# Two weight sums made by an accumulating DMA, and seven products in ten of sixteen weight pairs

## The chip, the cores and the metric

The kernel runs on one core of a Trainium2 chip. The metric is the device time of one execution in microseconds (us). The core has five instruction queues that this text names as the profile does: PE (matmuls), DVE and ACT (element-wise work), POOL and SP (which here mostly start DMAs). Each queue runs its instructions in the order in which the program holds them; an instruction that has to wait holds up everything behind it on its queue.

## What is computed

One encoder layer on 256 frames of 4096 channels: a layer norm, one wide projection, a retention branch and a forgetting-attention branch, a gated merge, an output projection and a last layer norm. Cut to what costs time:

```
h = layer_norm(x, ln_in_g, ln_in_b)                       # 256 x 4096
proj = h @ w_in                                           # 4096 x 24592, most of the work
q_r, k_r, v_r, g_r, q_f, k_f, v_f, g_f, f, gates = split(proj)
y_r = group_norm(retention(rotary(q_r), rotary(k_r), v_r)) * silu(g_r)
y_f = forgetting_attention(q_f, k_f, v_f, f + b_forget) * silu(g_f)
merged = sigmoid(gates0) * (y_r @ w_branch_ret) + sigmoid(gates1) * (y_f @ w_branch_fox)
out = layer_norm(2**0.25 * h + merged @ w_out, ln_post_g, ln_post_b)
```

All is float32. The kernel splits each operand of a large product into a high and a low float32r part and adds three matmuls: high times high, high times low, low times high (`three`, L197 to L200).

## The kernel before

**The column pairs.** 20480 of the projection's columns are done as 20 column pairs of 1024 columns each (L885 to L888). For one column pair the 4096 channels are run through in 16 steps of 256. The code calls such a step a pair: two blocks of 128 channels by two blocks of 512 columns, so four weight blocks of 128 x 512, which the code calls b11, b12, b21 and b22; the other operand is two blocks of 128 channels by two of 128 frames.

**Eight or seven products.** A plain pair takes eight block products of three matmuls each, 24 matmuls. The pairs in `SEVEN` (8 to 15) use Winograd's form of Strassen's scheme: seven products, 21 matmuls, but with four sums of activation blocks, made once (`make_sops`, L361), and four sums of weight blocks, made anew for every pair and column pair by DVE: `ta` holds t1 and t3 (L184, one instruction of 1024 columns), `tb` holds t2 and t4 (L186 and L187, 512 columns each). Each sum is then split, the high part by an ACT cast and the low part by a DVE subtraction (`split_into`, L152), into the tile `tset`. Three more splits are needed for the raw blocks. The products add up in eight PSUM tiles over the 16 pairs; then ACT copies them out (`proj_evac`, L389) and DVE combines them (`combine`).

**Buffers.** Weights come as one DMA of 1 MB for each pair, issued by SP into one of three `wraw` buffers (`u_load`, L133). The split blocks lie in two sets of slots, used in turn, the sums' parts in two `tset` tiles, used in turn (yb0 and yb1). The activation sums of eight pairs fill yb2 and yb3.

**Order.** `PAIRS` takes a plain and a seven-product pair in turn: 0, 8, 1, 9 and so on. The code issues the splits of a pair as soon as the slots it needs are free in the code's own reckoning (`feed`, `slots_for`), and the next load after that (`load_more`). A list scheduler then sets each queue's final order, so matmuls of neighbouring pairs stand interleaved.

Of the kernel before, what the change touches and what calls it, by code (L numbers as in the profile page):

```python
# [8 lines left out]
F32 = mybir.dt.float32  # L9
# [4 lines left out]
P = 128  # L14
# [15 lines left out]
SEVEN = tuple(range(8, 16))  # L30
GATE0, GATE1 = 7, 15
PAIRS = tuple(p for i in range(8) for p in (i, 8 + i))
# [3 lines left out]
def hybrid_kernel(  # L36
# [29 lines left out]


    xt = []
    for t in range(T):
        xt.append(big.tile([P, D], F32, name=f"x{t}", tag=f"yb{t}"))  # L70
# [86 lines left out]
    def u_split(u):  # L157
# [15 lines left out]
        B = [raw[:, i * NC:(i + 1) * NC] for i in range(4)]  # L173
        st = [tuple(w_tile(s_, i) for i in range(2)) for s_ in u["slots"][:2]]
        if not u["seven"]:
            for i in range(2):
                split_into(st[i][0], st[i][1], raw[:, 2 * i * NC:2 * (i + 1) * NC])
            u["b"] = [(st[i // 2][0][:, i % 2 * NC:(i % 2 + 1) * NC], st[i // 2][1][:, i % 2 * NC:(i % 2 + 1) * NC])
                      for i in range(4)]
            return  # L180
        split_into(st[0][0], st[0][1], raw[:, NC:3 * NC])
        ta = work.tile([P, 2, NC], F32, name="ta", tag="w4a", bufs=1)
        tb = work.tile([P, 2, NC], F32, name="tb", tag="w4b", bufs=1)
        nc.vector.tensor_tensor(ta, B[0][:, None, :].to_broadcast([P, 2, NC]),  # L184
                                raw[:, NC:3 * NC].rearrange("p (a n) -> p a n", a=2), op=ALU.add)
        nc.vector.tensor_tensor(tb[:, 0, :], ta[:, 0, :], B[2], op=ALU.add)  # L186
        nc.vector.tensor_tensor(tb[:, 1, :], tb[:, 0, :], B[3], op=ALU.add)  # L187
        split_into(st[1][0][:, :NC], st[1][1][:, :NC], B[3])
        ts = big.tile([P, 2, 2, 2, NC], F32R, name="tset", tag="yb0" if u["slots"][2] == "t0" else "yb1")
        for i, t_ in enumerate((ta, tb)):  # L190
            split_into(ts[:, i, 0], ts[:, i, 1], t_)
        two = lambda x, i: (x[0][:, i * NC:(i + 1) * NC], x[1][:, i * NC:(i + 1) * NC])
# [24 lines left out]
    def pair_pe(u):  # L217
# [11 lines left out]
        if u["seven"]:  # L229
# [3 lines left out]
            work_ = [("1", blk(0, 0), f["b11"]), ("2", blk(0, 1), f["b21"]), ("6", so(2), f["t2"]),  # L233
                     ("5", so(1), f["t1"]), ("3", so(0), f["b22"]), ("7", so(3), f["t3"]), ("4", blk(1, 1), f["t4"])]
# [126 lines left out]
    def make_sops(hi, lo, pairs_, sops):  # L361
        sh = big.tile([P, len(pairs_), 4, P], F32R, name="soh", tag="yb2")
# [765 lines left out]
```

## Time and profile before

| | us |
|---|---|
| median of 3 runs | 2848.74 (2847.06 to 2856.11) |
| the profiled execution, its own time | 2845.76 |
| its span, from first to last instruction | 2844.0 |
| PE busy | 2793.1 (98%) |
| DVE busy | 2305.3 (81%) |
| ACT busy | 1565.1 (55%) |
| POOL busy | 169.8 (6%) |

The column pairs take the stretch from about 131 to 1749 us, 57% of the span. The granted TensorE clock is 1.00 there, the higher of its two levels. A matmul's own duration (0.39 us) is longer than the distance to the next one, since they overlap; what a matmul costs is read from how many start in a stretch.

### The profile page before, as it was taken

The numbers are of one execution on the slowest core, as the hardware profiler recorded it, in microseconds if no ns is written. First come the engines' busy times: TensorE is split into PE (matmuls) and PEld (weight loads), VectorE is DVE, ScalarE is ACT, GpSimd is POOL, SyncE is SP. The second block draws the span as 40 slices with busy tenths as digits, with TensorE's granted clock in tenths as the row PEclk, the third lists the DMA queues.
The fourth block names the chain that finished last, engine by engine and source line by source line (L and its number), as shares of the span: only waits on it lengthen the run. The fifth ranks groups of instructions, "written<-read, shape, count | busy, mean of one in ns | idle before, by whom it ended". The sixth has DMA issues, their size and how long they took to land. (4 is left out here: it accounts for less than half of the span.)

```text
span 2844.0 us, 34687 instructions
## 1 busy us (share of the span) xinstructions
PE 2793.1 (98%) x12666; PEld 2308.8 (81%) x12666; DVE 2305.3 (81%) x2988; ACT 1565.1 (55%) x2170; POOL 169.8 (6%) x302
## 2 busy tenths in 40 slices
PE   7999999999999999999999999999999999999998
PEld 5788888888887887888878888788898888888886
DVE  7899999998999988989889888877675656656666
ACT  5565666656555655555555565445664444444443
POOL 1000000000000000000000000212220000000000
PEclk9999999999999999999999999999999999999999
DMA  6556655665566655556656656866676566666564
GB/s 221 198 207 239 225 219 214 230 224 205 214 222 222 222 211 211 211 211 222 222 213 218 221 204 224 290 229 202 204 232 216 211 215 211 226 215 231 210 233 170
DMA packets 128156, 620.28 MB, mean 218 GB/s; under 512 B 15803, under 2 KB 16075, under 8 KB 87019
## 3 DMA queue, kind: packets, MB, share of 16 engines
q1 hardware_dynamic: 105552, 543.47, 52.8%
q0 software_dynamic: 21856, 72.49, 8.2%
q8 instruction: 99, 1.62, 0.2%
q10 hardware_dynamic: 576, 2.10, 0.2%
q14 instruction: 73, 0.60, 0.1%
HBM read 588.54 MB, written 29.46 MB: 217 GB/s over the span
## 5 line engine op out<-in xcount | busy, mean ns | idle before, releaser
L153 ACT CAST whi<-wraw 128x1024 fp32r<-128x1024 f32 (+1 forms) x640 | 586.3, 945 | 373.7 <-PE ps L200 262.1
L154 DVE TENSOR_TENSOR wpart<-wraw,wpart 128x512 fp32r<-128x512 f32 (+2 forms) x790 | 520.4, 667 | 314.0 <-ACT wpart L153 311.9
L153 ACT CAST wpart<-wraw 128x512 fp32r<-128x512 f32 (+2 forms) x790 | 475.3, 606 | 525.5 <-DVE wpart L154 314.4
L154 DVE TENSOR_TENSOR wlo<-wraw,whi 128x1024 fp32r<-128x1024 f32 (+1 forms) x640 | 680.8, 1084 | 8.7 <-ACT whi L153 7.2
L199 PE MATMUL ps<-wlo,hTh 128*128 128x512 f32 x960 | 373.7, 389 | 0.0
L200 PE MATMUL ps<-whi,hTl 128*128 128x512 f32 x960 | 373.4, 389 | 0.0
L198 PE MATMUL ps<-whi,hTh 128*128 128x512 f32 x960 | 340.2, 390 | 5.8 <-ACT ev L397 5.6
L184 DVE TENSOR_TENSOR ta<-wraw 128x1024 f32<-128x1024 f32 x160 | 195.6, 1222 | 137.6 <-DMA wraw<-in_w_in 136.5
L153 ACT CAST tset<-tb 128x1024 fp32r<-128x1024 f32 x160 | 169.3, 1058 | 183.8 <-DVE tb L187 183.6
L199 PE MATMUL acc<-wlo,hTh 128*128 128x512 f32 x640 | 249.1, 391 | 3.4 <-DVE wlo L154 3.4
L200 PE MATMUL acc<-whi,hTl 128*128 128x512 f32 x640 | 247.8, 389 | 0.0
L198 PE MATMUL acc<-whi,hTh 128*128 128x512 f32 x640 | 242.2, 389 | 0.4 <-ACT whi L153 0.4
L153 ACT CAST tset<-ta 128x1024 fp32r<-128x1024 f32 x160 | 167.6, 1048 | 120.1 <-DVE ta L184 119.8
L198 PEld LDWEIGHTS ps<-whi,hTh 128*128 128x128 f32 x960 | 180.2, 188 | 46.4 <-ACT ev L397 9.1
L199 PE MATMUL acc<-wpart,hTh 128*128 128x512 f32 (+2 forms) x568 | 212.2, 377 | 4.2 <-DVE wpart L154 4.1
L200 PEld LDWEIGHTS ps<-whi,hTl 128*128 128x128 f32 x960 | 180.2, 188 | 37.6
L199 PEld LDWEIGHTS ps<-wlo,hTh 128*128 128x128 f32 x960 | 180.2, 188 | 37.3
L200 PE MATMUL acc<-wpart,hTl 128*128 128x512 f32 (+2 forms) x568 | 208.2, 370 | 0.6 <-DVE rstd L96 0.6
L154 DVE TENSOR_TENSOR tset<-tb,tset 128x1024 fp32r<-128x1024 f32 x160 | 195.0, 1219 | 4.7 <-ACT tset L153 4.7
L154 DVE TENSOR_TENSOR tset<-ta,tset 128x1024 fp32r<-128x1024 f32 x160 | 194.8, 1217 | 0.4
L199 PE MATMUL acc<-wpart,mTh 128*128 128x512 f32 x500 | 194.6, 389 | 0.0
L200 PE MATMUL acc<-wpart,mTl 128*128 128x512 f32 x500 | 194.5, 389 | 0.0
(257 smaller groups left out, 4853.3 us busy)
## 6 DMA issues: line engine op xcount, KB each, us to landing
wraw<-in_w_in SPq DMA_DIRECT2D x320, 1024.0 KB, 4.9
wraw<-in_w_out SPq DMA_DIRECT2D x128, 512.0 KB, 4.1
wraw<-in_w_in SPq DMA_DIRECT2D x112, 512.0 KB, 4.8
wraw<-in_w_branch_ret SPq DMA_DIRECT2D x64, 512.0 KB, 4.2
wraw<-in_w_branch_fox SPq DMA_DIRECT2D x64, 512.0 KB, 4.2
proj_d<-ev POOLq DMA_DIRECT2D x64, 256.0 KB, 3.5
g<-gates_d POOLq DMA_DIRECT2D x16, 512.0 KB, 5.7
wraw<-in_w_in SPq DMA_DIRECT2D x16, 272.0 KB, 4.5
```

Source lines behind the costliest of these rows:

```text
L153: c = nc.scalar.copy(hi, src)
L154: nc.vector.tensor_tensor(lo, src, hi.bitcast(F32), op=ALU.subtract)
L184: nc.vector.tensor_tensor(ta, B[0][:, None, :].to_broadcast([P, 2, NC]), raw[:, NC:3 * NC].rearrange("p (a n) -> p a n", a=2), op=ALU.add)
L198: nc.tensor.matmul(o, lhsT=a[0], rhs=w[0], start=first, stop=False)
L199: nc.tensor.matmul(o, lhsT=a[0], rhs=w[1], start=False, stop=False)
L200: return nc.tensor.matmul(o, lhsT=a[1], rhs=w[0], start=False, stop=last)
```

## The change

Four things change together.

- Ten of the sixteen pairs (6 to 15) go by seven products, and `PAIRS` becomes 0, 6, 7, 1, 8, 9, 2, 10, 11, 3, 12, 13, 4, 14, 5, 15, so that seven-product pairs often follow each other.
- The sum `ta` is no longer made by DVE. The four weight blocks of such a pair are stored in another order. SP loads three of them (768 KB) into `wraw`; a second DMA on SP writes the fourth twice, side by side, into one half of a new tile `mix`; and an accumulating DMA on POOL adds two of the blocks, fetched again from memory, to it there.
- There is one `tset` instead of two, and its tile stays the same all along, so its quarters are released one by one. The seven products now start with those that use the sums (5, 7, 6, 4) and end with 1, 3, 2.
- The buffer that this frees, yb1, is cut in two: one half holds the activation sums of the two added pairs, the other holds `mix`, which is two `ta` buffers used in turn. `tb` gets two buffers too.

```diff
-SEVEN = tuple(range(8, 16))
+SEVEN = tuple(range(6, 16))
-PAIRS = tuple(p for i in range(8) for p in (i, 8 + i))
+PAIRS = (0, 6, 7, 1, 8, 9, 2, 10, 11, 3, 12, 13, 4, 14, 5, 15)
...
     def u_load(ld):
         raw = wp.tile([P, 4 * NC], F32, name="wraw", tag="wraw", bufs=RAW)
         w = ld["srcs"][0].shape[0] // P
+        if ld.get("seven"):
+
+            src = ld["srcs"][0].rearrange("(p f) -> p f", p=P)
+            nc.sync.dma_start(raw[:, :3 * NC], src[:, :3 * NC])
+            ta = scr["ta"][scr["n"] % 2]
+            scr["n"] += 1
+            nc.sync.dma_start(ta, src[:, None, 3 * NC:].to_broadcast([P, 2, NC]))
+            nc.gpsimd.dma_start(ta, src[:, :2 * NC].rearrange("p (a n) -> p a n", a=2), accum_op=ALU.add)
+            ld["raw"], ld["ta"] = raw, ta
+            return
...
-        split_into(st[0][0], st[0][1], raw[:, NC:3 * NC])
-        ta = work.tile([P, 2, NC], F32, name="ta", tag="w4a", bufs=1)
-        tb = work.tile([P, 2, NC], F32, name="tb", tag="w4b", bufs=1)
-        nc.vector.tensor_tensor(ta, B[0][:, None, :].to_broadcast([P, 2, NC]),
-                                raw[:, NC:3 * NC].rearrange("p (a n) -> p a n", a=2), op=ALU.add)
-        nc.vector.tensor_tensor(tb[:, 0, :], ta[:, 0, :], B[2], op=ALU.add)
-        nc.vector.tensor_tensor(tb[:, 1, :], tb[:, 0, :], B[3], op=ALU.add)
-        split_into(st[1][0][:, :NC], st[1][1][:, :NC], B[3])
-        ts = big.tile([P, 2, 2, 2, NC], F32R, name="tset", tag="yb0" if u["slots"][2] == "t0" else "yb1")
+        ta, ts = u["ld"]["ta"], scr["t"]
+        tb = work.tile([P, 2, NC], F32, name="tb", tag="w4b" if scr["s"] % 2 else "w4a", bufs=1)
+        scr["s"] += 1
+        nc.vector.tensor_tensor(tb[:, 0, :], ta[:, 0, :], raw[:, NC:2 * NC], op=ALU.add)
+        nc.vector.tensor_tensor(tb[:, 1, :], tb[:, 0, :], raw[:, 2 * NC:3 * NC], op=ALU.add)
         for i, t_ in enumerate((ta, tb)):
             split_into(ts[:, i, 0], ts[:, i, 1], t_)
+        split_into(st[0][0], st[0][1], raw[:, :2 * NC])
+        split_into(st[1][0][:, :NC], st[1][1][:, :NC], raw[:, 2 * NC:3 * NC])
...
-            work_ = [("1", blk(0, 0), f["b11"]), ("2", blk(0, 1), f["b21"]), ("6", so(2), f["t2"]),
-                     ("5", so(1), f["t1"]), ("3", so(0), f["b22"]), ("7", so(3), f["t3"]), ("4", blk(1, 1), f["t4"])]
+            work_ = [("5", so(1), f["t1"]), ("7", so(3), f["t3"]), ("6", so(2), f["t2"]), ("4", blk(1, 1), f["t4"]),
+                     ("1", blk(0, 0), f["b11"]), ("3", so(0), f["b22"]), ("2", blk(0, 1), f["b21"])]
...
-        sh = big.tile([P, len(pairs_), 4, P], F32R, name="soh", tag="yb2")
-        sl = big.tile([P, len(pairs_), 4, P], F32R, name="sol", tag="yb3")
+        so = [big.tile([P, 4, 2, 4, P], F32R, name="sop", tag=f"yb{2 + i}") for i in range(2)]
+        so.append(big.tile([P, 2, 2, 4, P], F32R, name="sop2", tag="yb1a"))
+        mix = big.tile([P, 4, NC], F32, name="mix", tag="yb1b")
+        scr["ta"] = mix[:, 0:2], mix[:, 2:4]
+        scr["t"] = big.tile([P, 2, 2, 2, NC], F32R, name="tset", tag="yb0")
...
         while state["loaded"] < min(len(loads), state["done"] + RAW):
+            if loads[state["loaded"]].get("seven") and "ta" not in scr:
+                break
             u_load(loads[state["loaded"]])
...
-            cands = [("r0", "r1") if (i - first_pair) % 2 else ("a0", "a1")]
             if u["seven"]:
-                state["t"] = state.get("t", 0)
-                cands = [c + ("t" + str(state["t"] % 2),) for c in cands]
+                cands = [c + ("t",) for c in cands]
```

Other tiles that used yb1 as a whole (x, yrl, z) are now two half tiles behind a small class that picks the half.

**SP's queue.** In the middle of the column pairs SP's queue held one load for each pair; the number in a name tells buffers apart, and the bracket names what a row waits for: DVE's semaphore (the last reader of the buffer), and earlier DMAs on SP (DMAHW) or on POOL (DMASW).

```order
L137 DMA wraw_12829<-in_w_in 128x2048 [waits DMAHW7_49,DVE_49]
L137 DMA wraw_12864<-in_w_in 128x2048 [waits DMAHW0_49,DVE_49]
L137 DMA wraw_12907<-in_w_in 128x2048 [waits DMAHW1_49,DVE_49]
L137 DMA wraw_12941<-in_w_in 128x2048 [waits DMAHW2_49,DVE_49]
L137 DMA wraw_12982<-in_w_in 128x2048 [waits DMAHW3_49,DVE_49]
```

Now seven-product pairs have two rows, L160 for three blocks and L163 for the doubled fourth block, and plain pairs one (L168).

```order
L160 DMA wraw_12168<-in_w_in 128x1536 [waits DMAHW5_49,DMAHW1_49,DVE_49]
L163 DMA mix_798<-in_w_in 128x2x512 [waits DMASW1_49,DVE_49]
L160 DMA wraw_12235<-in_w_in 128x1536 [waits DMAHW2_49,DVE_49]
L168 DMA wraw_12247<-in_w_in 128x2048 [waits DMAHW4_49,DMAHW0_49,DVE_49]
L163 DMA mix_798<-in_w_in 128x2x512 [waits DMASW5_49,DVE_49]
L160 DMA wraw_12287<-in_w_in 128x1536 [waits DMAHW5_49,DVE_49,Activation_49]
L163 DMA mix_798<-in_w_in 128x2x512 [waits DMAHW3_49,DMASW6_49,DVE_49]
```

The DVE instruction that each L163 waits for is the low-part subtraction of `ta` two seven-product pairs earlier, the last reader of that half of `mix`.

**DVE's queue.** A seven-product pair (wraw_12864) beside a plain one (wraw_12829) before: L184 makes `ta`, L186 and L187 make `tb`, L154 are the low parts.

```order
L184 TENSOR_TENSOR ta_12970<-wraw_12864 128x1024
L154 TENSOR_TENSOR tset_12902<-tb_12896,tset_12902 128x1024
L154 TENSOR_TENSOR wlo_12934<-wraw_12829,whi_12933 128x1024
L154 TENSOR_TENSOR tset_12977<-ta_12970,tset_12977 128x1024
L186 TENSOR_TENSOR tb_12971<-ta_12970,wraw_12864 128x512
L154 TENSOR_TENSOR wlo_12936<-wraw_12829,whi_12935 128x1024
L154 TENSOR_TENSOR wlo_12967<-wraw_12864,whi_12966 128x512
L187 TENSOR_TENSOR tb_12971<-tb_12971,wraw_12864 128x512
```

Now the seven-product pair with wraw_12235, behind the plain pair's first low part (wraw_12247): L214 and L215 make `tb`, L185 are the low parts.

```order
L185 TENSOR_TENSOR wlo_12340<-wraw_12235,whi_12339 128x1024
L185 TENSOR_TENSOR wlo_12342<-wraw_12235,whi_12341 128x512
L185 TENSOR_TENSOR wlo_12359<-wraw_12247,whi_12358 128x1024
L214 TENSOR_TENSOR tb_12343<-mix_798,wraw_12235 128x512
L185 TENSOR_TENSOR wlo_12361<-wraw_12247,whi_12360 128x1024
L185 TENSOR_TENSOR tset_799<-mix_798,tset_799 128x1024
L215 TENSOR_TENSOR tb_12343<-tb_12343,wraw_12235 128x512
```

The row that made `ta` is gone; L214 now waits for the accumulating DMA instead, and the half of `mix` that it reads is released two rows behind it, by the L185 on mix_798.

## Rows read from the trace of the kernel before

**Rows 1.** Page: span, busy time, and the chain that ended last.

```profile
span 2844.0 us, 34687 instructions
PE 2793.1 (98%) x12666; PEld 2308.8 (81%) x12666; DVE 2305.3 (81%) x2988; ACT 1565.1 (55%) x2170; POOL 169.8 (6%) x302
...
PE 26%; DVE 0%; ACT 0%; DVEq 0%; issue 0%
```

**Rows 2.** Windows: engines' busy us (x instructions), PEclk, DMA share, GB/s.

```profile
300.00:400.00 100.00, 100.00 (x443) 82.81 (x442) 94.30 (x104) 62.11 (x74) 5.20 (x10) 1.00 0.64 228
400.00:404.00 4.00, 4.00 (x20) 3.30 (x19) 4.00 (x5) 1.19 (x2) 0.00 (x0) 1.00 1.03 420
...
131.00:1749.00 1618.00, 1604.35 (x7033) 1317.93 (x7032) 1467.61 (x1578) 951.26 (x1109) 45.67 (x84) 1.00 0.60 217
```

**Rows 3.** Timeline of ACT: first copy-out of the first and last column pair.

```profile
204.29 0.58 ACT L397 COPY ev<-ps 128x512 f32<-128x512 f32 x1
...
1773.25 0.58 ACT L397 COPY ev<-ps 128x512 f32<-128x512 f32 x1
```

**Rows 4.** Groups by line and shape: count, busy us, mean ns, idle before.

```profile
L184 DVE TENSOR_TENSOR ta<-wraw 128x1024 f32<-128x1024 f32 x160 | 195.6, 1222 | 137.6 <-DMA wraw<-in_w_in 136.5
L154 DVE TENSOR_TENSOR tset<-ta,tset 128x1024 fp32r<-128x1024 f32 x160 | 194.8, 1217 | 0.4
...
L153 ACT CAST tset<-ta 128x1024 fp32r<-128x1024 f32 x160 | 167.6, 1048 | 120.1 <-DVE ta L184 119.8
```

**Rows 5.** Timeline of DVE: start, duration; the distance between starts counts.

```profile
128.15 0.67 DVE L154 TENSOR_TENSOR wlo<-wraw,whi 128x512 fp32r<-128x512 f32 x1
128.75 0.67 DVE L154 TENSOR_TENSOR sol<-so,soh 128x512 fp32r<-128x512 f32 x1
129.35 1.21 DVE L154 TENSOR_TENSOR wlo<-wraw,whi 128x1024 fp32r<-128x1024 f32 x1
130.49 0.67 DVE L154 TENSOR_TENSOR sol<-so,soh 128x512 fp32r<-128x512 f32 x1
```

**Rows 6.** DMA issues: queue, count, KB each, median us from issue to landing.

```profile
wraw<-in_w_in SPq DMA_DIRECT2D x320, 1024.0 KB, 4.9
wraw<-in_w_out SPq DMA_DIRECT2D x128, 512.0 KB, 4.1
...
g<-gates_d POOLq DMA_DIRECT2D x16, 512.0 KB, 5.7
...
rab<-proj_d POOLq DMA_DIRECT2D x8, 512.0 KB, 6.7
...
xc<-in_x POOLq DMA_DIRECT2D x8, 512.0 KB, 5.0
...
gates_d<-g POOLq DMA_DIRECT2D x6, 512.0 KB, 7.4
```

**Rows 7.** SP's 512 KB weight loads of L137, 2400 to 2700 us.

```profile
DMA to landing us min/median/max: 3.1/4.1/7.1
```

**Rows 8.** POOL's 512 KB loads of L466 (qk, v and gates of the branches).

```profile
DMA to landing us min/median/max: 4.0/6.0/8.9
```

**Rows 9.** Waits: who waited for whom, us in total, times, longest.

```profile
DVE ta L184 <- DMA wraw<-in_w_in: 136.5, 93, 2.6
...
PE ps L198 <- ACT ev L397: 5.6, 7, 1.4
```

More of the change, by code (lines that the diff above doesn't have):

```diff
@@ L65, in bcast, with __init__, __getitem__, big1 @@
         return ap1[n0:n0 + n].rearrange("(o n) -> o n", o=1).to_broadcast([P, n])
+    class Halves:
+        def __init__(self, a, b, half):
+            self.t, self.half = (a, b), half
+        def __getitem__(self, key):
+            p, c, *rest = key
+            h = self.half
+            if isinstance(c, slice):
+                i = c.start // h
+                c = slice(c.start - i * h, c.stop - i * h)
+            else:
+                i, c = divmod(c, h)
+            return self.t[i][(p, c, *rest)]
+    def big1(shape, dt, name):
+        half = [P, shape[1] // 2] + shape[2:]
+        return Halves(*[big.tile(half, dt, name=name + e, tag="yb1" + e) for e in "ab"], shape[1] // 2)
     xt = []
     for t in range(T):
-        xt.append(big.tile([P, D], F32, name=f"x{t}", tag=f"yb{t}"))
+        xt.append(big1([P, D], F32, "x1") if t else big.tile([P, D], F32, name="x0", tag="yb0"))
     for t in range(T):
@@ L128, in add_pair @@
         for i, p in enumerate(order):
-            loads.append(dict(n=4 * NC, srcs=[take(wname, 4 * P * NC)], users=1))
+            loads.append(dict(n=4 * NC, srcs=[take(wname, 4 * P * NC)], users=1, seven=p in sops))
             units.append(dict(kind="p", ld=loads[-1], p=p, seven=p in sops, hi=hi, lo=lo, sops=sops, g=i,
                               ng=len(order), evac=evac, h=holder, drain=False, pre=None))
+    scr = dict(n=0, s=0)
     def u_load(ld):
@@ L171, in u_split @@
             return
-        B = [raw[:, i * NC:(i + 1) * NC] for i in range(4)]
         st = [tuple(w_tile(s_, i) for i in range(2)) for s_ in u["slots"][:2]]
@@ L361, in make_sops @@
     def make_sops(hi, lo, pairs_, sops):
-        sh = big.tile([P, len(pairs_), 4, P], F32R, name="soh", tag="yb2")
-        sl = big.tile([P, len(pairs_), 4, P], F32R, name="sol", tag="yb3")
+        so = [big.tile([P, 4, 2, 4, P], F32R, name="sop", tag=f"yb{2 + i}") for i in range(2)]
[3 more added lines that the diff above has]
+        scr["t"] = big.tile([P, 2, 2, 2, NC], F32R, name="tset", tag="yb0")
         for n_, p in enumerate(pairs_):
-            sops[p] = (sh[:, n_], sl[:, n_])
+            hl = so[n_ // 4][:, n_ % 4]
+            sops[p] = (hl[:, 0], hl[:, 1])
         yield
@@ L376, in make_sops @@
             nc.vector.tensor_tensor(o[:, 0, :], a12, o[:, 2, :], op=ALU.add)
-            split_into(sh[:, n_], sl[:, n_], o)
+            split_into(*sops[p], o)
             yield
@@ L483, in retention @@
         yr["h"] = big.tile([P, 16, S], F32R, name="yrh", tag="yb0")
-        yr["l"] = big.tile([P, 16, S], F32R, name="yrl", tag="yb1")
+        yr["l"] = big1([P, 16, S], F32R, "yrl")
         def fetch_qk(gi):
@@ L805, in pre @@
                 for t in range(T):
-                    z[t] = big.tile([P, D], F32, name=f"z{t}", tag=f"yb{t}")
+                    z[t] = big1([P, D], F32, "z1") if t else big.tile([P, D], F32, name="z0", tag="yb0")
                 bg.append(post_rows())
@@ L934, in slots_for @@
             if all(q not in user or last_step[user[q]] < s_ for q in c):
-                if u["kind"] == "p" and u["seven"]:
-                    state["t"] += 1
                 return c
@@ L1061, in pairs_of @@
     v = w.reshape(k // (2 * P), 2, P, n // (2 * NC), 2, NC)[:, :, :, :, ::-1]
-    v = v.transpose(3, 0, 2, 1, 4, 5)[:, list(order)]
+    v = v.transpose(3, 0, 2, 1, 4, 5)[:, list(order)].reshape(n // (2 * NC), len(order), P, 4, NC)
+    v = np.stack([v[:, i][:, :, [1, 2, 3, 0]] if p in SEVEN else v[:, i] for i, p in enumerate(order)], axis=1)
     return np.ascontiguousarray(v).reshape(-1)
```

## The prediction

> **What bounds the kernel now.** I read the page's busy times and chain first, then windows over the column pairs, then the waits. PE is busy for 98% of the span and is nearly all that the chain names [rows 1]. In 300 to 400 us it runs 443 matmuls without a gap, so one costs 0.2257 us, at a granted clock of 1.00 [rows 2]. A column pair has 8 x 24 + 8 x 21 = 360 matmuls, 81.25 us. From its first copy-out to that of the last, 19 column pairs take 1568.96 us, 82.6 each [rows 3]: some 1.3 us of each goes to waits. DVE is next, busy 1467.61 of 1618 us in that stretch, 0.91; the DMA engines are at 0.60 and 217 GB/s [rows 2]. So the stage is PE's, with DVE close behind. Loads cost PE nothing: DVE waits 136.5 us for them before it makes `ta` [rows 4, 9], but has the time back before PE wants the parts.
>
> **What the change takes off.** Two more seven-product pairs save three matmuls each: 120 over 20 column pairs, 120 x 0.2257 = 27.1 us if PE stays the bound. On DVE a wide instruction (1024 columns) costs 1.14 us and a narrow one (512) 0.60, by the distance between starts [rows 5]; the means of 1.22 [rows 4] overlap. A seven-product pair took four wide and three narrow ones, 6.36 us, and takes three and three now, 5.22; a plain pair takes two wide, 2.28. With eight combining sums that is 8 x 6.36 + 8 x 2.28 + 4.8 = 73.9 us per column pair before and 10 x 5.22 + 6 x 2.28 + 4.8 = 70.7 after: by its work DVE is no bound.
>
> **What costs nothing.** One `tset` instead of two: the cast of the next `ta` waits for products 5 and 7 of the pair before, behind which its 6, 4, 1, 3 and 2 stand, 15 matmuls or 3.4 us; cast and subtraction take 1.05 + 1.22 = 2.27 [rows 4]. Without that cover it would be 2.27 us at each of the four places in a column pair where two such pairs touch, 182 us in all. The activation sums of two added pairs are made while the first chunks run, some 4 us of DVE that PE does not wait for; at worst these 4 us. The last pair of a column pair now ends with 1, 3 and 2, while ACT still copies out x, 1, 2 first: PE waited 1.4 us at most for a copy-out, 5.6 in all [rows 9], so 0 to 28 us; I take 0, since the next pair can begin with x.
>
> **The wait that is added.** `ta` now comes by three hand-overs: SP may write the doubled block into a half of `mix` only when DVE has read that half for the last time, in the subtraction of `ta` two seven-product pairs earlier; POOL may start the add only when that has landed; DVE may start `tb` only when the add has landed. What stands behind the waiting L214 on DVE in the order (a low part of the plain pair, the subtraction of `ta`) is what PE needs next. Let L be the time from the start of the doubled load to the landing of the add. The chain through one half of `mix` then closes on itself in every column pair. For the half that serves pairs 7, 9, 11, 13 and 15 the order has, from each L214 to the subtraction that releases the half, both counted: 4 wide and 13 narrow rows (pair 7, where the combining sums stand between), 5 and 3, 2 and 1, 4 and 3, 1 and 1. That is 16 wide and 21 narrow, 18.2 + 12.6 = 30.8 us, and five L. DVE has to do them in this order, and some wait for their ACT cast: at the busy share of 0.91 [rows 2] the 30.8 would be 33.9. I take 33. A column pair cannot be shorter than 33 + 5 L; the other half of `mix` has 24.4 us of DVE rows and is slacker. L that just fits into the 82.6 of before is 9.9 us; to have all of the 27 us it must be under 9.6.
>
> **How long is L?** No row shows an accumulating DMA, so I bound its two parts. The doubled load is 512 KB on SP, and stands right behind a 768 KB one: 512 KB loads land after 3.1 us at least and 4.1 in the median [rows 7], a whole 1 MB after 4.9 [rows 6]. I take 4.1, bounds 3.1 and 4.9. The add is 512 KB issued from POOL: plain loads of that size there land after 4.0 us at least [rows 8], 5.0, 5.7 and 6.7 in the median of three groups, and the slowest group of that size takes 7.4 [rows 6]. The add also has to fetch the old 512 KB; on SP 1 MB takes 0.8 us longer than 512 KB (4.9 against 4.1, rows 6). I take the middle group with that, 5.7 + 0.8 = 6.5, bounds 4.0 and 7.4. So L is 10.6, bounds 7.1 and 12.3.
>
> The Trainium skill has a rule on this ("Collectives: The Full Stack", section on the bandwidth ceiling): an add in the DMA engines is slow not by its arithmetic but because it reads two sources, and ran at about half the rate of a copy there. No row here shows it. By that rule a second 512 KB at the best rate of rows 2 (1.25 us at 420 GB/s) stands in the place of my 0.8: L 11.05, a column pair 88.3 and 2962 in all, inside the range of my own case.
>
> **The sum.** 33 + 5 x 10.6 = 86.0 us for a column pair against 82.6: 3.4 x 20 = +68 us. The saved matmuls are in it, since PE with 354 of them (79.9 us) then waits. 2845.76 + 68 is 2914 for the profiled execution, which lay 3 us under the median: 2917.
>
> **The rivals.**
>
> *The add is hidden.* If L is near the lowest rows, 3.1 + 4.0 = 7.1, the chain needs 68.5 us and PE stays the bound: 2848.7 - 27.1 = 2822. For it: the order leaves PE other matmuls to do while parts are late, the DVE is relieved, and the DMA engines idle for 0.4 of the stage. Against it: such landings are the fastest in their groups, and here the queues are fuller.
>
> *The DMA engines fill up.* A seven-product pair moves 768 + 512 + 512 KB and fetches the old 512 KB: 2.36 MB against 1.05. Ten of those, six plain pairs and the 1.05 MB of stores are 30.9 MB for each column pair, against 17.8. At the best rate of rows 2 (420 GB/s) that is 74 us of 82.6, at the stage's mean (217 GB/s at 0.60, so 362) it is 85. Then each landing takes what its slower rows show, L = 4.9 + 7.4 = 12.3, and a column pair 94.5: +238 us, 3087.
>
> *Both cancel.* L of 9.7 to 10.0: the chain just takes what PE saves, within 8 us of 2849.
>
> **Chances.** A time within 0.3% (8.5 us) of the old one is what a measurement of this kernel cannot tell from no change. Chain through the add longer than the saving, L from 10.0 to 11.6, 2857 to 3020: 0.44, and this range is that case's own. DMA engines full, above that: 0.18. Hidden: 0.28. Cancelled: 0.10. So faster 0.28, same 0.10, slower 0.62. The range reaches from just under the hidden case, 2815, to 3060 inside the full one, and leaves out about 2 in 10, mostly at the top.
>
> **What would show it.** In the profile after: L164 issue-to-landing near 6.5 us and L163 near 4.1 (under 8.5 together, or over 12, and I am wrong in the one direction or the other); DVE idle before L214 put down to the DMA into mix, well over the 136.5 us of before; PE idle in the column pairs, put down to tset; copy-outs 86 us apart; DMA share near 0.8. If copy-outs come under 82 us apart, the wait is hidden. If PE waits for copy-outs or for `tset` at adjacent pairs with the adds long landed, I costed those at nothing and was wrong there.

## The result, and the profile after

The changed kernel takes 3424.49 us (median of 4 runs, 3420.55 to 3436.94) against 2849.77 for the kernel before on the same chip: a ratio of 1.2032, 95% interval 1.2007 to 1.2056. It is slower, as forecast, but by 575 us and not by 68, and beyond the range.

Page after; it answers to [rows 1]:

```profile
span 3423.6 us, 35605 instructions
PE 2975.4 (87%) x12546; PEld 2383.7 (70%) x12546; DVE 2257.6 (66%) x3000; ACT 1630.0 (48%) x2252; POOL 342.8 (10%) x502
...
PE 15%; issue 6%; DVE 1%; DMA 0%; POOL 0%; ACT 0%; DVEq 0%; POOLq 0%
```

The 120 matmuls are gone (12546 for 12666), and no engine is full any more. The windows after, with the columns of [rows 2]:

```profile
131.00:2300.00 2169.00, 1769.64 (x6900) 1384.15 (x6899) 1414.21 (x1588) 1012.16 (x1187) 214.93 (x280) 0.91 0.83 232
...
600.00:1600.00 1000.00, 820.92 (x3208) 642.79 (x3207) 651.07 (x725) 467.93 (x547) 99.07 (x129) 0.91 0.84 235
1004.00:1008.00 4.00, 0.00 (x0) 0.00 (x0) 0.00 (x0) 0.00 (x0) 0.85 (x1) 1.00 1.04 218
...
1012.00:1016.00 4.00, 4.00 (x12) 3.11 (x11) 4.00 (x5) 0.92 (x2) 0.00 (x0) 0.55 0.28 78
```

The first two show it over nearly all of the column pairs and over 1 ms of them: DVE at 0.65, the DMA engines at 0.83 and 0.84 for 0.60 before, yet with only 232 and 235 GB/s for 217. The last two show one wait close up: for 4 us no engine computes, while the DMA engines are full and move only 218 GB/s, where the same share moved 420 before [rows 2]. Behind this idle stretch the granted clock is 0.55 of 2.4 GHz, near the lower level of 1.2 GHz: PE, busy throughout, starts 12 matmuls in 4 us where it started 20 before [rows 2]. From 600 to 1600 us there are 3208 matmuls, so the 354 of a column pair take 110.3 us. The copy-outs agree (timeline of ACT; it answers to [rows 3]): from the first to the last, 19 column pairs take 2115.67 us, 111.4 each, for 82.6.

```profile
235.31 0.58 ACT L429 COPY ev<-ps 128x512 f32<-128x512 f32 x1
...
2350.98 0.57 ACT L429 COPY ev<-ps 128x512 f32<-128x512 f32 x1
```

DMA issues after, as in [rows 6]:

```profile
wraw<-in_w_in SPq DMA_DIRECT2D x200, 768.0 KB, 6.3
wraw<-in_w_in SPq DMA_DIRECT2D x120, 1024.0 KB, 6.8
mix<-in_w_in SPq DMA_DIRECT2D x200, 512.0 KB, 7.4
mix<-in_w_in POOLq DMA_DIRECT2D x200, 512.0 KB, 7.6
```

The doubled load lands after 7.4 us where 4.1 was taken, the add after 7.6 where 6.5 was: L is 15.0 us and not 10.6. The whole raw loads, too, land later, after 6.8 us for 4.9. The waits answer to [rows 9]:

```profile
POOL mix L164 <- DMA mix<-in_w_in: 1200.7, 139, 17.3
DVE tb L214 <- DMA mix<-in_w_in: 469.4, 129, 11.3
ACT tset L184 <- DMA mix<-in_w_in: 420.0, 104, 11.0
ACT tset L184 <- PE ps L228: 394.9, 136, 9.5
...
PEld acc L227 <- DVE tset L185: 204.7, 84, 8.7
PE acc L227 <- DVE tset L185: 171.3, 61, 8.3
```

Read from the top, this is the added chain, link by link: POOL waits for the doubled load, DVE and ACT for the add, PE for `tset`. The link that closes it into a loop stands in SP's own waits: 194 of the 200 doubled loads wait for the subtraction that releases their half of `mix`.

```profile
SPq L163 <- DVE tset L185: 332.6, 194, 9.9
```

One pass through one half, from a doubled load to the next one into the same half (timelines of SP, POOL and DVE):

```profile
1015.95 0.38 SPq L163 DMA_DIRECT2D mix<-in_w_in  x1
...
1022.63 0.84 POOL L164 DMA_DIRECT2D mix<-in_w_in  x1 [4.62 <-DMA mix<-in_w_in]
...
1028.90 0.69 DVE L214 TENSOR_TENSOR tb<-mix,wraw 128x512 f32<-128x512 f32 x1 [2.76 <-DMA mix<-in_w_in]
...
1035.86 1.22 DVE L185 TENSOR_TENSOR tset<-mix,tset 128x1024 fp32r<-128x1024 f32 x1
...
1037.11 0.38 SPq L163 DMA_DIRECT2D mix<-in_w_in  x1
```

The next load starts 0.03 us after the subtraction ends, and it does so in every pass from 600 to 1600 us. In the half that serves pairs 7, 9, 11, 13 and 15 a pass takes 22.05 us in the mean of that stretch: 7.3 for the doubled load, 0.6 until POOL starts the add, 7.4 for the add, 0.3 until DVE starts `tb`, and 6.4 from there to the end of the subtraction.

### The profile page after: what moved, and what is told of

Its sections match the earlier page's. It is cut to its first block, busy times and chain, and to the rows that moved or that the text cites. A ratio compares the mean times of both kernels' runs of the same rounds, so it can differ in the third digit from the quotient of the medians.

```text
span 3423.6 us, 35605 instructions
## 1 busy us (share of the span) xinstructions
PE 2975.4 (87%) x12546; PEld 2383.7 (70%) x12546; DVE 2257.6 (66%) x3000; ACT 1630.0 (48%) x2252; POOL 342.8 (10%) x502
## 3 DMA queue, kind: packets, MB, share of 16 engines
q0 software_dynamic: 50656, 177.36, 24.3%
## 5 line engine op out<-in xcount | busy, mean ns | idle before, releaser
L185 DVE TENSOR_TENSOR wpart<-wraw,wpart 128x512 fp32r<-128x512 f32 (+2 forms) x790 | 520.8, 668 | 314.0 <-ACT wpart L184 311.4
L184 ACT CAST wpart<-wraw 128x512 fp32r<-128x512 f32 (+2 forms) x790 | 475.2, 606 | 526.3 <-DVE wpart L185 307.0
L185 DVE TENSOR_TENSOR wlo<-wraw,whi 128x1024 fp32r<-128x1024 f32 (+1 forms) x640 | 655.0, 1051 | 63.3 <-ACT whi L184 62.7
L184 ACT CAST whi<-wraw 128x1024 fp32r<-128x1024 f32 (+1 forms) x640 | 558.3, 913 | 252.8 <-PE ps L228 108.0
L214 DVE TENSOR_TENSOR tb<-mix,wraw 128x512 f32<-128x512 f32 x200 | 138.0, 690 | 623.3 <-DMA mix<-in_w_in 469.4
L184 ACT CAST tset<-mix 128x1024 fp32r<-128x1024 f32 x200 | 209.8, 1049 | 641.0 <-DMA mix<-in_w_in 420.0
L227 PE MATMUL ps<-wlo,hTh 128*128 128x512 f32 x720 | 297.2, 413 | 88.3 <-DVE wlo L185 88.2
L164 POOL DMA_DIRECT2D mix<-in_w_in x200 | 171.0, 855 | 1758.2 <-DMA mix<-in_w_in 1200.7
L227 PE MATMUL acc<-tset,sop 128*128 128x512 f32 x400 | 180.0, 450 | 171.3 <-DVE tset L185 171.3
L184 ACT CAST tset<-tb 128x1024 fp32r<-128x1024 f32 x200 | 210.4, 1052 | 244.8 <-PE ps L228 181.2
L226 PE MATMUL ps<-whi,hTh 128*128 128x512 f32 x720 | 290.3, 413 | 16.0 <-ACT whi L184 15.0
L228 PE MATMUL ps<-whi,hTl 128*128 128x512 f32 x720 | 292.9, 407 | 0.0
L185 DVE TENSOR_TENSOR tset<-mix,tset 128x1024 fp32r<-128x1024 f32 x200 | 243.9, 1220 | 72.0 <-ACT tset L184 72.0
L185 DVE TENSOR_TENSOR tset<-tb,tset 128x1024 fp32r<-128x1024 f32 x200 | 243.8, 1219 | 9.0 <-ACT tset L184 8.4
L227 PEld LDWEIGHTS acc<-tset,sop 128*128 128x128 f32 x400 | 82.7, 207 | 218.8 <-DVE tset L185 204.7
L227 PEld LDWEIGHTS acc<-wlo,hTh 128*128 128x128 f32 x640 | 132.6, 207 | 133.1 <-DVE wlo L185 105.2
```

The lines of the kernel that those rows point to most:

```text
L164: nc.gpsimd.dma_start(ta, src[:, :2 * NC].rearrange("p (a n) -> p a n", a=2), accum_op=ALU.add)
L184: c = nc.scalar.copy(hi, src)
L185: nc.vector.tensor_tensor(lo, src, hi.bitcast(F32), op=ALU.subtract)
L214: nc.vector.tensor_tensor(tb[:, 0, :], ta[:, 0, :], raw[:, NC:2 * NC], op=ALU.add)
L226: nc.tensor.matmul(o, lhsT=a[0], rhs=w[0], start=first, stop=False)
L227: nc.tensor.matmul(o, lhsT=a[0], rhs=w[1], start=False, stop=False)
```

## The experiments

A period below is the time of one column pair: its matmuls (354 with ten seven-product pairs, 357 with nine, 360 with eight) over the count in the window from 600 to 1600 us. Engine time is the period times the DMA share: what all 16 DMA engines spend on one column pair. The kernel before has 360 / 4349 ms = 82.8 us on this measure and 2840 to 2841 us in the runs beside the experiments. Each profile line with a window is that stretch, its columns as in [rows 2]; runs without an interval were run once.

**Are the other parts to blame? e3 and e16.** All stays but the way `ta` is made:

```diff
-            nc.sync.dma_start(raw[:, :3 * NC], src[:, :3 * NC])
+            nc.sync.dma_start(raw, src)
...
-            nc.sync.dma_start(ta, src[:, None, 3 * NC:].to_broadcast([P, 2, NC]))
-            nc.gpsimd.dma_start(ta, src[:, :2 * NC].rearrange("p (a n) -> p a n", a=2), accum_op=ALU.add)
...
+        nc.vector.tensor_tensor(ta, raw[:, None, 3 * NC:].to_broadcast([P, 2, NC]),
+                                raw[:, :2 * NC].rearrange("p (a n) -> p a n", a=2), op=ALU.add)
```

> Ten pairs by seven products, the new orders and the single tset stay; the first two sums are made by VectorE into the half of mix, from a raw tile of four blocks, and no second or third transfer is issued; the result is the reference's. Theory: VectorE's work for a column pair is 70.7 + 10 x 1.14 = 82.1 us, about the pitch of 82.6 before, and the matmuls need 81.2: 2820 to 2880 us. Rival A: the same, as the bytes of before are moved. Rival B (the other parts cost it): over 3100.

2863.71 us, ratio 1.0082 (1.0066 to 1.0099). Its window:

```profile
600.00:1600.00 1000.00, 986.67 (x4290) 799.76 (x4289) 994.50 (x1091) 622.16 (x727) 26.02 (x48) 1.00 0.59 217
```

The same with SEVEN and PAIRS of the kernel before (eight pairs, alternating):

> Eight pairs by seven products in the alternating order with one tset and the new order of products, the first two sums on VectorE into the halves of mix, no second or third transfer; the result is the reference's. It is the kernel of the 3086 us run with only the sums moved. If the transfers are that run's whole loss: 2835 to 2870 us, as the kernel before within 1 per cent. If one tset and the order of products are part of it: 2900 or more.

2850.23 us. So the single `tset`, the order of products and the touching pairs cost nothing that shows at ten pairs beyond VectorE's work (busy 994.50 of 1000 us); at eight, where no pairs touch, the first two cost some 0.3%, from one run. The loss is in the two transfers.

**What each transfer costs: e1, e2, e17.** Three edits of the changed kernel. In e1 the add is left out:

```diff
-            nc.gpsimd.dma_start(ta, src[:, :2 * NC].rearrange("p (a n) -> p a n", a=2), accum_op=ALU.add)
```

> The accumulating DMA is left out and all else of the changed kernel stays, so ta holds the last block twice and the products that use it are not the reference's. Theory (the loop through one half of mix, 33 us + 5 times the sum's time, where the sum is the doubled load and the add, 7.4 + 7.6 = 15.0 us): only the doubled load is left, 33 + 5 x 7.4 = 70 us at most for a column pair, below what the matrix engine needs, so 2805 to 2860 us. Rival A (the DMA engines are full: share 0.83 to 0.85 through the pairs): the add's engine time goes as well, so also below 2900. Rival B (the other parts of the change, the single tset, the order of the products or of the pairs, cost it): above 3200, since they all stay.

3019.98 us, a miss for every theory. Window, and the landing of the doubled load:

```profile
600.00:1600.00 1000.00, 924.00 (x3802) 717.70 (x3801) 778.53 (x864) 551.60 (x648) 23.84 (x44) 0.98 0.68 221
```

```profile
mix<-in_w_in SPq DMA_DIRECT2D x200, 512.0 KB, 5.9
```

Without the add, the order of instructions came out otherwise, and made another loop. Timeline of e1:

```profile
1011.64 0.69 DVE L213 TENSOR_TENSOR tb<-mix,wraw 128x512 f32<-128x512 f32 x1 [2.70 <-DMA mix<-in_w_in]
...
1012.98 1.22 DVE L184 TENSOR_TENSOR tset<-mix,tset 128x1024 fp32r<-128x1024 f32 x1
...
1014.23 0.38 SPq L163 DMA_DIRECT2D mix<-in_w_in  x1
...
1020.41 0.69 DVE L213 TENSOR_TENSOR tb<-mix,wraw 128x512 f32<-128x512 f32 x1 [0.47 <-DMA mix<-in_w_in]
...
1021.02 1.22 DVE L184 TENSOR_TENSOR tset<-mix,tset 128x1024 fp32r<-128x1024 f32 x1
...
1022.26 0.38 SPq L163 DMA_DIRECT2D mix<-in_w_in  x1
```

DVE makes the first sum of a pair and, behind it, the subtraction of the pair before, which releases the other half; SP issues the next load as soon as that ends, and 6 us later the next first sum starts: here each load waits for the sum before it, so all ten stand in one row, 93.1 / 10 = 9.3 us each. It is no measure of the loop in the changed kernel; of the doubled load it is one: 5.9 us with no add running.

In e2 it is a plain overwrite:

```diff
-            nc.gpsimd.dma_start(ta, src[:, :2 * NC].rearrange("p (a n) -> p a n", a=2), accum_op=ALU.add)
+            nc.gpsimd.dma_start(ta, src[:, :2 * NC].rearrange("p (a n) -> p a n", a=2))
```

> The GpSimd DMA of the same 512 KB into the same half of mix stays, with all its waits, but overwrites in place of adding; ta is then two plain blocks and the result is not the reference's. Theory (the loop, L = 15.0 because the add takes twice the engine time of a copy and slows the other transfers): both transfers fall to 4 to 5.5 us, L = 8 to 11, 33 + 5 L = 73 to 88 us for a column pair against 112.2, so 2820 to 2960 us. Rival A (full DMA engines): 85 per cent of 112.2 = 95 us of engine time for a column pair, less 10 times 1.75 us that the adding costs over copying = 78 us, so 2820 to 2900 as well; told from the theory by the time from issue to landing, which would stay near 7. Rival B (the other parts): 3424, nothing of them changes.

3257.23 us, outside the ranges of the theory and of both rivals; landings 6.8 (doubled load) and 5.6 us (overwrite), window:

```profile
600.00:1600.00 1000.00, 859.63 (x3434) 671.20 (x3433) 698.66 (x781) 499.87 (x584) 73.55 (x137) 0.94 0.76 251
```

L is 12.4, more than expected, and the period 103.1. Engine time is 78.3 us here, 63.3 in e1 and 110.3 x 0.84 = 92.7 in the changed kernel: a plain 512 KB from POOL takes 1.50 us of all engines, an adding one 2.94. POOL's queue by itself gives the same: its packets take 24.3% of the changed kernel's span, 16.7% of e2's and 7.8% of e1's (section 3 of the pages), so 2.98 us for an adding transfer and 1.54 for a plain one.

In e17 the doubled load takes 4 KB rows:

```diff
-            nc.sync.dma_start(ta, src[:, None, 3 * NC:].to_broadcast([P, 2, NC]))
+            nc.sync.dma_start(ta, src[:, 2 * NC:].rearrange("p (a n) -> p a n", a=2))
```

> The changed kernel with the doubled load replaced by a load of two different blocks, the third and the fourth, that lie beside each other, into the same half of mix: the same 512 KB written, each partition's 4 KB from one row in place of 2 KB read twice (ta is then not the reference's sum). The add and all waits stay. If the form of the doubled load makes it slow (7.4 us, and 5.9 us where no add ran, against 4.1 for 512 KB of w_out): it falls to about 6, the loop is 5 x (6 + 7.3 + 7.5) = 104 us for a column pair, 3240 to 3320 us. If it is the fuller engines alone: 7 us and more, 3390 to 3450.

3286.63 us, as expected from the form; landings 6.5 and 6.6 us, window:

```profile
600.00:1600.00 1000.00, 854.84 (x3409) 662.61 (x3409) 690.16 (x770) 496.99 (x584) 103.21 (x134) 0.94 0.84 248
```

Period 103.8, L 13.1, engine time 87.2: reading a 2 KB row twice costs 0.55 us of engine time more than a 4 KB row, and delays both landings by 0.9 to 1.0.

**Loop or engines? e4, e13, e5.** In e4 the doubled load and the add still run, but VectorE makes `ta` in w4a from a whole raw tile; e13 is e4 without the two transfers.

```diff
+        ta = work.tile([P, 2, NC], F32, name="ta", tag="w4a", bufs=1)
...
-        tb = work.tile([P, 2, NC], F32, name="tb", tag="w4b" if scr["s"] % 2 else "w4a", bufs=1)
+        tb = work.tile([P, 2, NC], F32, name="tb", tag="w4b", bufs=1)
```

> As the run in which VectorE makes the first two sums (into the work tile w4a, tb alone in w4b), but the doubled load and the accumulating DMA are still issued into the halves of mix for every pair by seven products, and nothing reads them: the same traffic as the changed kernel and 256 KB more for each such pair, and no compute instruction that waits for it. Theory (the loop through mix): 2830 to 2950 us. Rival A (full DMA engines set the pace): at least 95 us of engine time for a column pair, 19 x (95 - 82.6) = 236 us over the kernel before, so 3080 or more. Rival B: as the run without the transfers, whatever that is, and over 3100.

3278.79 us, with this window:

```profile
600.00:1600.00 1000.00, 845.55 (x3309) 641.90 (x3308) 782.03 (x845) 476.88 (x563) 116.67 (x150) 0.94 0.94 283
```

> Ten pairs by seven products, the first two sums on VectorE into the work tile w4a and tb always in w4b, no transfer into mix: the run with the idle transfers, without them; the result is the reference's. If the traffic of the idle transfers alone cost that run its time: 2850 to 2900 us, as with the sums in the two halves (2864). If the single tiles for ta and tb are part of what the runs with idle, with half and with two transfers paid: 2940 us or more, and those runs show less of the transfers than it seemed.

2923.87 us, between its two forecasts. So single tiles for `ta` and `tb` cost 60 us (against e3), and transfers that nobody reads 355 more: the share is 0.94 and whole raw loads land after 9.8 us. The time lies in rival A's range, although no compute instruction waits for a sum made by DMA. It is not free of chains, though. A doubled load still waits for the add before it in the same half, 1228 us in all, and the raw loads share its queue (SP's own waits, and L163 by itself):

```profile
SPq L163 <- DMA mix<-in_w_in: 1228.0, 194, 13.6
...
L163 SPq DMA_DIRECT2D mix<-in_w_in x200: 368/379/1267, 59.0 to 1849.6; - x100
```

The transfers also run ahead of the pairs that they belong to: the last is issued at 1849.6 us, and from about 1940 us on the last three column pairs take 85 to 88 us each, as in e13 (86). How much of the 355 us is engine time and how much SP's wait, e4 does not separate.

In e5 the changed kernel gets a third buffer, with the loads issued as soon as one is free (`tb` has a single tile then):

```diff
+        third = work.tile([P, 2, NC], F32, name="mix3", tag="w4a", bufs=1)
+        scr["ta"] = mix[:, 0:2], mix[:, 2:4], third
...
+        while "ta" in scr and scr["n"] < min(len(sevens), scr["s"] + 3):
```

> The changed kernel with a third buffer for the first two sums (the work tile w4a; tb then alone in w4b), its loads issued as soon as a buffer is free; same bytes, same sums, the result is the reference's. Theory 1 (the loop of load, add and reader through two buffers sets 112.2 us for a column pair): with three, 2/3 of it, 75 us, so the matrix and vector engines bind, 2840 to 2950 us. Theory 2 (DMA engine time sets a floor): the changed kernel spends 0.84 x 110 = 93 us of all 16 engines' time on a column pair, and with the idle transfers these reached a share of 0.94 at most, so 93 / 0.94 = 99 us, 19 x (99 - 82.6) = 310 us over the kernel before: 3100 to 3250 us. Theory 3 (the single tset and the matrix engine's order hold the readers back): no change, 3380 or more.

3182.9 us, theory 2's forecast: 241 less than with two halves, though L rose to 17.8 (8.9 and 8.9):

```profile
600.00:1600.00 1000.00, 889.79 (x3577) 693.05 (x3576) 728.61 (x809) 514.36 (x608) 108.73 (x141) 0.94 0.92 261
```

So both are there. Two halves made a loop of 110 us; with three, an add has landed 7.9 us (in the mean of the window) before DVE starts to read it. Behind the loop stands engine time, 91 us of a period of 99.0, and what waits now is ScalarE, for raw loads (372.6 us from 300 to 1700 us). That engine time alone holds this kernel is not shown; e9 below speaks against it.

**The same at eight pairs: e7, e15, e18, e14.** e7 takes SEVEN and PAIRS from the kernel before:

```diff
-SEVEN = tuple(range(6, 16))
-PAIRS = (0, 6, 7, 1, 8, 9, 2, 10, 11, 3, 12, 13, 4, 14, 5, 15)
+SEVEN = tuple(range(8, 16))
+PAIRS = tuple(p for i in range(8) for p in (i, 8 + i))
```

> Eight pairs by seven products in the old alternating order of pairs, so none follows another; the accumulating DMA, the single tset and the order of the products stay; the result is the reference's. Theory 1 (loop): four sums through each half, 33 + 4 x 15 = 93 us, and less where the transfers land sooner: 2900 to 3060 us. Theory 2 (DMA engine time): 48.7 + 8 x 4.4 = 84 us of engine time, at a share of 0.94 at most 89 us for a column pair: 2970 or more. Theory 3 (pairs by seven products that follow each other, with one tset): 2850 to 2880, as nothing follows now.

3085.57 us, just above theory 1's range and inside theory 2's; landings 7.8 and 6.9:

```profile
600.00:1600.00 1000.00, 924.75 (x3886) 737.66 (x3885) 717.03 (x781) 524.89 (x608) 99.03 (x131) 0.98 0.89 262
```

e15 gives it four halves, in the space that eight pairs leave in yb1a, and issues as e5 does:

```diff
+        mix2 = big.tile([P, 4, NC], F32, name="mix2", tag="yb1a")
...
+        scr["ta"] = mix[:, 0:2], mix[:, 2:4], mix2[:, 0:2], mix2[:, 2:4]
```

> Eight pairs by seven products in the alternating order with the doubled load and the accumulating DMA (3086 us with two halves), and four halves for the sums, issued as soon as one is free; tb alternates as in the changed kernel; the result is the reference's. Engine time was 0.89 x 92.6 = 82 us for a column pair. If the loop through two halves held it: the share rises to 0.92 to 0.95, 87 to 90 us for a column pair, 2930 to 3000 us. If the engines' time holds it already at 0.89: 3050 to 3100.

2953.17 us, as forecast for the loop; landings 8.6 and 9.2:

```profile
600.00:1600.00 1000.00, 965.08 (x4159) 779.42 (x4158) 765.46 (x831) 554.89 (x641) 104.43 (x138) 0.99 0.94 279
```

e18 is e15 with the overwrite of e2.

> Eight pairs by seven products and four halves of mix (2953 us), with the GpSimd DMAs overwriting in place of adding (the products that use ta are not the reference's); bytes and waits stay. If the engines' time sets that run (81.4 us for a column pair at a share of 0.94): without the reading of the old value 8 x 1.4 = 11 us less, 70 us at 0.94 = 75, so no longer the bound, and the kernel comes to 2845 to 2885 us, near the one with the sums on VectorE (2850). If the loop, the queues or the number of transfers do: 2920 or more.

2912.07 us, a little above the band of the engines' theory, below the other's; landings 8.3 and 7.2:

```profile
600.00:1600.00 1000.00, 973.34 (x4239) 793.05 (x4238) 780.10 (x846) 571.75 (x661) 75.15 (x140) 1.00 0.87 284
```

With eight pairs the steps follow each other, from one run each: 2850 without the transfers (e16), 62 more for two plain ones through four halves (e18), 41 for the adding (e15), 132 for having two halves in place of four (e7).

e14 is e7 with a fourth raw tile in yb1a:

```diff
+        scr["raw"] = big.tile([P, 4 * NC], F32, name="wraw4", tag="yb1a")
...
+        if "raw" in scr and ld["n"] == 4 * NC and scr["l"] % 4 == 1:
+            raw = scr["raw"]
```

> Eight pairs by seven products in the alternating order with the doubled load and the accumulating DMA (3086 us with three raw tiles), and a fourth raw tile in the space that eight pairs leave free, so a raw load can be issued one pair earlier; the result is the reference's. If the raw loads, slowed to 6 to 8 us and with only three tiles ahead, hold VectorE and ScalarE: 2920 to 3020 us. If the DMA engines' time is what is short (share 0.89): no gain, 3060 or more. If the loop through the two halves of mix is: no gain either, and the waits of the first sum on mix stay.

3207.91 us, worse, where every theory had a gain or none; landings 7.9 and 8.0:

```profile
600.00:1600.00 1000.00, 880.72 (x3579) 699.27 (x3578) 654.79 (x719) 486.55 (x557) 90.27 (x119) 0.94 0.81 241
```

A longer lead of the raw loads is no cure. The time from `tb`'s start to the release of a half rose from 5.9 to 8.5 us (means of the window), and the add landed later too; why is not shown.

The kernels with two halves that share the loop can be laid beside each other. Each half is used five times in a column pair (four in e7 and e14); L is the sum of the two median landings:

| kernel | period, us | time per use | L | time less L |
|---|---|---|---|---|
| changed | 110.3 | 22.1 | 15.0 | 7.1 |
| e2, plain overwrite | 103.1 | 20.6 | 12.4 | 8.2 |
| e17, 4 KB rows | 103.8 | 20.8 | 13.1 | 7.7 |
| e7, eight pairs | 92.6 | 23.2 | 14.7 | 8.5 |
| e14, fourth raw tile | 100.6 | 25.1 | 15.9 | 9.2 |

L moves by 3.5 us and the rest by 2.1. In e15 a use takes 43.3 us with L 17.8, in e5 29.7: there the loop has slack, and the add has landed 19.5 and 7.9 us before DVE starts to read it.

**Three plain buffers: e9.** e5 with the overwrite of e2.

> The kernel with three buffers for the first two sums, its GpSimd DMAs overwriting in place of adding (the products that use ta are not the reference's); bytes and waits stay. Theory (DMA engine time sets the pace with three buffers): with the plain copy the changed kernel spent 0.76 x 103.1 = 78 us of the 16 engines' time on a column pair, against 93 with the add, and three buffers let the share reach 0.92, so 78 / 0.92 = 85 us: 19 x (85 - 82.6) = 46 us over the kernel before, 2860 to 2920 us. Rival (a loop through the buffers, the tset or the queues holds the run with three buffers at 99 us, and the share of 0.92 is a coincidence): 3050 or more.

3080.98 us: neither. The period is 93.6 us at a share of 0.81:

```profile
600.00:1600.00 1000.00, 922.18 (x3783) 729.00 (x3781) 768.98 (x856) 541.40 (x640) 80.66 (x151) 0.96 0.81 276
```

Neither the engines nor the loop (28.1 us per use, L 13.8) are full. `tb` has a single tile here, which cost 60 us at most in e13. ScalarE still waits 313.8 us for raw loads (300 to 1700 us), and in the same stretch the doubled loads, which share SP's queue with them, wait 421 us there for DVE. Whether that queue's order holds the raw loads back was not tested with three buffers; the rest is open, and e10 and e12 meet it again.

**Can a part of it pay? e6, e10, e12, e11, e8.** In e6 every second seven-product pair takes its `ta` from the DMAs, the others from VectorE (into w4a, as in e13); e10 is e6 with the doubled load on POOL's queue; in e12 only two of ten pairs use the DMAs (`% 5` for `% 2`).

```diff
+            scr["k"] += 1
+            if scr["k"] % 2:
+                nc.sync.dma_start(raw, src)
+                return
```

> Of the ten pairs by seven products, every second has its first two sums made by the doubled load and the accumulating DMA, the others by VectorE into the work tile w4a; the result is the reference's. Theory 1 (loop): five sums through two halves, 2.5 x (15 + 7) = 55 us for a column pair, hidden; VectorE's work is 70.7 + 5 x 1.14 = 76.4 us and the matmuls need 79.9: 2810 to 2850 us, at or below the kernel before. Theory 2 (DMA engine time): 48.7 + 5 x 4.4 = 71 us of engine time for a column pair, below 82.6 but a share of 0.86, at which loads take 6 to 7 us: 2830 to 2950. Theory 3 (tset and the orders): as the run with the sums on VectorE, 2864.

3062.52 us (3046.02 to 3072.47), ratio 1.0777 (1.0738 to 1.0815), outside all three ranges: theory 1's hidden loop gained nothing.

> The kernel in which every second pair by seven products has its first two sums made by DMA, with the doubled load issued on GpSimd's queue, ahead of the accumulating DMA, in place of SyncE's; the result is the reference's. Theory (SyncE takes its issues in order, so a raw load stands behind a doubled load that waits for the half's last reader, and that costs this kernel 92.8 us for a column pair at a DMA share of only 0.77): without it 83 to 87 us, 2850 to 2930. Rival (the DMA engines in bursts, with only three raw tiles): as with SyncE, 3020 to 3080.

3048.64 us: the rival. It is 14 us under e6's median and inside the range of e6's own runs, so SyncE's order is worth little or nothing here.

> Ten pairs by seven products, the first two sums of eight of them on VectorE and of two by the doubled load and the accumulating DMA; the result is the reference's. VectorE 82.1 - 2 x 1.14 = 79.8 us for a column pair, the matmuls 79.9; DMA engine time 48.7 + 2 x 4.4 = 57.5 us, a share of 0.71. If the busier engine sets it: 2810 to 2845 us. If even two waits of SyncE's queue on a half's reader delay the raw loads: 2870 to 2930.

2981.16 us, ratio 1.0498 (1.0480 to 1.0515), above both ranges. Beside e13, which has the same single tiles (2924), two sums by DMA in a column pair cost 57 us, five 139 (e6), and ten, read by nobody, 355 (e4): 29, 28 and 35 us for each, the first two although every such sum spares VectorE 1.14 x 20 = 23 us. At a share of 0.65 the DMA engines are not full in e12, and L is still 13.1:

```profile
wraw<-in_w_in SPq DMA_DIRECT2D x280, 1024.0 KB, 5.1
...
mix<-in_w_in SPq DMA_DIRECT2D x40, 512.0 KB, 6.3
mix<-in_w_in POOLq DMA_DIRECT2D x40, 512.0 KB, 6.8
```

ScalarE waits 277 us for raw loads there and 187 in e13 (360 in e6). That is where the time shows; what delays these loads at such a share is not settled.

e11 is e3 with nine seven-product pairs (SEVEN from 7, PAIRS reordered):

> Nine pairs by seven products, the first two sums on VectorE into the half of mix, one tset, no accumulating DMA; the result is the reference's. Between the eight of the kernel before and the ten that ran at 2864: VectorE 78 us for a column pair, the matmuls 357 x 0.2257 = 80.6 us against 81.2 before. If the busier of the two engines sets it: 2815 to 2840 us. If one tset with pairs that follow each other holds the readers back: 2845 or more.

2841.8 us, ratio 1.0000 (0.9991 to 1.0009), between the two forecasts.

```profile
600.00:1600.00 1000.00, 998.85 (x4398) 824.14 (x4397) 964.78 (x1046) 616.76 (x718) 25.97 (x48) 1.00 0.60 220
```

PE is busy 99.9% of the window, and a column pair takes 357 / 4398 ms = 81.2 us there, for 82.8. So the saved matmuls show in the middle and not in the whole: from the first copy-out to the last, the column pairs are 13 us shorter than in the profile of the kernel before, and the time ahead of them and behind them is 10 us longer; why is not shown. e8 is e3 with `combine` on GpSimd (`nc.gpsimd.tensor_tensor` for `nc.vector.tensor_tensor`):

> The kernel with ten pairs by seven products and the first two sums on VectorE, with the combining of the eight products (8 to 11 sums of 128x512 for a column pair) moved from VectorE to GpSimd; the result is the reference's. VectorE was 99 per cent busy there, at 82.5 us for a column pair; without these sums (0.60 us of each) it needs 76 to 77 us, and the matmuls 79.9. If VectorE was what bound it: 2805 to 2835 us, below the kernel before. If GpSimd's sums slow VectorE's by sharing memory, or hold up its DMA issues: 2850 or more.

3005.98 us, ratio 1.0579 (1.0560 to 1.0598): with GpSimd's sums beside them VectorE's instructions take longer, and VectorE is busy 967 us of the window although it makes fewer sums. Groups of e8 by form, in the window:

```profile
L182 DVE TENSOR_TENSOR wlo<-wraw,whi 128x1024 fp32r<-128x1024 f32 x244 | 308.4, 1276 | 7.5 <-ACT whi L181 6.1 <-PE ps L227 1.2
L182 DVE TENSOR_TENSOR tset<-tb,tset 128x1024 fp32r<-128x1024 f32 x112 | 172.4, 1539 | 4.3 <-ACT tset L181 4.3
```

and of e3:

```profile
L182 DVE TENSOR_TENSOR wlo<-wraw,whi 128x1024 fp32r<-128x1024 f32 x268 | 323.1, 1217 | 0.0
L182 DVE TENSOR_TENSOR tset<-tb,tset 128x1024 fp32r<-128x1024 f32 x122 | 148.5, 1218 | 3.6 <-ACT tset L181 3.4
```

No version beat the kernel before.

## Why the prediction was wrong

- **The loop was right.** "A column pair cannot be shorter than 33 + 5 L": with the measured L that is 108 us, and 110.3 to 111.4 were measured. The links wait as named, the next load starts 0.03 us after the release, and a third buffer takes 241 us off. In the half that the prediction took, the reader's part, 33, is 5 x 6.4 = 32 in the trace. Not counted were the hand-overs from load to add and from add to reader, 0.6 and 0.3 us in each pass, some 4.5 us of a column pair.
- **The step that failed is the size of L**, 10.6 for 15.0, outside its bounds of 7.1 and 12.3. Most of it is the doubled load: 4.1 us, bounds 3.1 and 4.9, were taken from plain loads, and 7.4 came. It is outside even with no add running: 5.9 us in e1, where whole raw loads of 1 MB land after 5.1. Of the 3.3 us, the 2 KB rows are 0.9 (e17) and 1.5 go with the adds (7.4 for 5.9 in e1); the other 0.9 is not separated. The add, 6.5 with bounds 4.0 and 7.4, took 6.8 in e12 and 7.6 here: just past its bound, and not the main error. 4.4 us too little in L, five times in each of 20 column pairs, is 440 of the 507 us missed.
- **The price of adding was read from the wrong pair of rows.** "The old 512 KB" was put at 0.8 us, from the landings of two plain loads. Against the overwrite of e2 the add lands 2.0 us later (7.6 for 5.6) and takes 1.44 us more of all the engines' time, as much as a copy (2.94 for 1.50). The Trainium skill ("Collectives: The Full Stack", section on the bandwidth ceiling), which the prediction weighed, says that an add reads two sources and ran at about half a copy's rate there; in engine time these runs agree. By that rule the sum was 2962, still far short, since it says nothing on the doubled load.
- **The full engines were a rival and are a part of the answer.** "74 us of 82.6" or 85 of engine time is 92.7, and the L of 12.3 from "what its slower rows show" was too low: whole raw loads land after 4.9 us at a share of 0.60, 6.8 at 0.84, 9.3 at 0.94 (e15). Loop and engines were priced as two cases; they work together, since the loop takes each slower landing five times. The share alone does not set L: it is 13.1 at 0.84 (e17) and 15.9 at 0.81 (e14). Once the loop is opened (e5) the kernel still takes 3183 at a share of 0.92, and with less engine time 3081 at 0.81 (e9), so engine time is not all that is left.
- **What was costed at nothing** held: one `tset` and the new orders (e3, e16). ACT waits 394.9 us for PE before `tset` casts, but e3, with the same tile and VectorE full, runs at 2864. VectorE's 70.7 us is 651.07 / 1000 x 110.3 = 71.8.
- **The 27.1 us of matmuls** came in no run: with the sums on VectorE, VectorE is full at ten pairs (e3), and at nine the whole kernel is no faster (e11).
- **The clock** at 0.91 was no step of the prediction, which priced every matmul at 1.00. In the stretch shown PE's clock is low behind an idle time; how much of the 575 us the clock adds is not separated.

## What to carry to other kernels

Before moving a sum into a DMA, multiply its time from issue to landing, measured on that very form, by how often a buffer goes round in the stage; with two buffers it is paid in full, and a third was worth 241 us here. Then add up engine time: here an adding transfer counted twice and a row read twice more than its bytes, and raw loads that had been hidden held ScalarE up for longer at a share of 0.65 already (277 us in e12, 187 in e13). A sum that spared VectorE 23 us over the column pairs cost some 28 us net (e6, e12).

## What the runs showed of the hardware

- 512 KB written by an accumulating DMA took 2.94 us of all 16 engines and 7.6 us to land (changed kernel), a plain one by the same queue 1.50 and 5.6 (e2).
- 512 KB from 2 KB rows read twice: 7.4 us to land, from 4 KB rows 6.5 (e17), in the same company; plain 512 KB loads before took 4.1 [rows 6].
- 128x512 sums on GpSimd lengthen VectorE's 128x1024 instructions from 1.22 to 1.28 us, and one group to 1.54 (e8).
- Behind an idle stretch of PE the granted clock was 0.55 from 1012 to 1016 us, and PE, busy throughout, started 12 matmuls in those 4 us, against 20 at 1.00 [rows 2] (changed kernel).
